# A hand-set order for TensorE in two attentions: what replacing a scheduler's order by set distances does to the time

## The chip, the cores and the metric

The kernel runs on one core of a Trainium2 chip. The metric is the device time of one execution in microseconds. Before the change it is 2630.18 us, the median of three runs (2629.49 to 2632.86). The profile shown below was taken of one further execution, which took 2629.03 us; the stretch from its first to its last instruction, the span, is 2627.2 us.

## The reference, cut to what matters

Two blocks of two layers each work on 512 latent tokens and 256 context tokens of width 1024. Only the first block's two attentions are touched by the change. In short form:

```python
# layer 0: neighborhood attention, 16 heads of 64
q, k = rms_norm(q, q_gain), rms_norm(k, k_gain)           # per head
s = concat(q @ k_window.T * dh**-0.5 + rpb_bias, q @ k_ctx.T * dh**-0.5)
y_lat = softmax(s) @ concat(v_window, v_ctx)              # 512 latent rows
y_ctx = softmax(q_ctx @ k_ctx.T * dh**-0.5) @ v_ctx       # 256 context rows

# layer 1: sliding window attention, 16 query heads on 4 key heads, with a sink
q, k = rope(rms_norm(q, g)), rope(rms_norm(k, g))
s = concat(where(|i - j| <= 128, q @ k.T, -1e30), q @ k_ctx.T, sink)
y_lat = softmax(s)[..., :-1] @ concat(v, v_ctx)
```

All of it is float32. Where a product needs more precision than one fast pass gives, a number is held as a high and a low part, and two or three fast products are summed.

## The kernel before, in words

Activations are kept with features on the partitions: `hl` (8 tiles of 128 features by 512 latent tokens) and `hc` (the same by 256 context tokens). After the norm their high and low parts are `uhl`, `ull`, `uhc`, `ulc`. A weight block arrives as `wraw` by DMA on SyncE's queue; `split` (L128, L129) makes `whi` on ScalarE and `wlo` on VectorE or, in the attentions, on GpSimd. A projection (`lin_steps`, L170; `tok_steps`, L180 for the values) is 24 products for a tile: high by high, high by low, and low by high. These are called dense products here, and their results are the tiles `mm`.

In the neighborhood attention the 16 heads are taken as 8 pairs (`hp`). `qk_proj` makes a pair's queries and keys in four tiles; `head_norm` squares a tile on ScalarE (L341), sums the squares with the matrix `blk` on TensorE into the tile `NS` (L344), takes logarithm, exponential and a square on ScalarE (L345, L346, L348), multiplies on GpSimd (L349) and corrects on VectorE (L350 to L352). There is one bank for `NS`, so the next `NS` product waits until L350 has read the last one. A pair has five blocks of 128 query rows (block 4 is the context), each for two heads; one such unit is `unit`: four score products into `S` (L391, L392), a softmax on VectorE and ScalarE (L358, L698 to L700), four transposes of the weights into `PT` (L704), and a copy into `pts` (L707 on ScalarE or L709 on VectorE). There is one `PT` bank. `attend` (L725) then makes the value products into `ST`, eight for a block.

In the sliding window attention `proj(t)` makes the queries of head pair `t`, `head_norm` follows, and `rope` turns them: a product with the matrix `rot` into the same `NS` bank (L820), which reads what L352 wrote. A unit here has scores against up to three blocks of keys (`SL`) and against the context (`SC`, one bank for both heads), a softmax (L358, L880 to L882), transposes into `PT` (L887), copies on ScalarE (L888), and value products (L904).

The order on every engine was set by the framework's scheduler. It takes instructions by priority, which is the order of the code, as soon as its own model of durations says that they are ready; the hardware then executes each engine's list strictly in that order. Only the `ada` bursts (products of the modulation weights, tile `AD`) were pinned behind a score product by hand.

Of the kernel before, what the change touches and what calls it, by code (L numbers as in the profile page):

```python
# [12 lines left out]
F32 = mybir.dt.float32  # L13
# [49 lines left out]
def kernel(ctx: ExitStack, tc: tile.TileContext, A, out, stop_after=None):  # L63
# [130 lines left out]

    def wide_w(w, c, s, **kw):

        return load_w([(0, 512, w[512 * s:512 * s + 512, c:c + 512])], 4, 512, **kw)
# [34 lines left out]
    def ada_burst(i, burst):  # L232

        for which, k, raw in burst:
# [4 lines left out]
            if k == KD - 1:  # L239
                ada_done(i, which, scr["adps"])  # L240

    def ada_done(i, which, ps, b=None):
# [4 lines left out]
        pt = bank(tag)  # L247
        n = 2 * nb
        for m in range(2):
            nc.tensor.matmul(out=pt[:, n * m:n * m + n], lhsT=rows[:, 128 * m:128 * m + 128], rhs=sel[:, n - 4:2 * n - 4])  # L250
# [7 lines left out]
        o = VOFF[f"ada_b{i}"][0]  # L258
        for v in range(2):
            nc.vector.tensor_tensor(  # L260
                out=view(mod[i][:, :, v]), in0=pt[:, 0:2 * n].rearrange("p (m j v) -> p m j v", v=2, j=nb)[:, :, :, v],
                in1=view(vecs[:, o:o + 48]), op=ALU.add)
# [74 lines left out]
    def head_norm(ps, n, gain):  # L337

        sq, r, q = tmp(n), tmp(n), tmp(n)
        ps = ps[:, :n]  # L340
        nc.scalar.activation(out=sq, in_=ps, func=AF.Square)  # L341
        nc.vector.tensor_scalar(out=q, in0=ps, scalar1=gain, scalar2=None, op0=ALU.mult)  # L342
        st = ns_tile()[:, :n]
# [84 lines left out]
    with tc.tile_pool(name="first", bufs=1) as fp, scratch("scr1", 6, 2):  # L428
# [154 lines left out]
        def neighborhood():  # L583
# [4 lines left out]
            with tc.tile_pool(name="na", bufs=1) as ap_:  # L588
# [26 lines left out]
                def qk_w(hp, lo_eng=None):  # L615
                    return load_w([(0, 128, wqkv[:, 128 * hp:128 * hp + 128]),
                                   (128, 128, wqkv[:, D + 128 * hp:D + 128 * hp + 128])], KD, 256, lo_eng)
# [47 lines left out]
                v_proj(0)  # L665

                def unit(hp, e, b):
# [18 lines left out]
                    else:  # L686
# [13 lines left out]
                        nc.vector.tensor_scalar(out=p, in0=p, scalar1=rl, scalar2=None, op0=ALU.mult)  # L700
                    pt = bank("PT")
# [3 lines left out]
                    pts = ap_.tile([128, 512], F32, name="pts", tag="pts", bufs=3)  # L705
# [4 lines left out]
                    return pts  # L710

# [31 lines left out]
                for hp in range(8):  # L743
                    pv = bank("ST")
                    if hp == 7:
                        scr["lo"] = nc.vector
                        oh = (u_lat(), u_ctx())
                    for b in range(5):
                        if b == 1 and hp < 7:
                            qk_proj(hp + 1, qk_w(hp + 1))  # L750
                        if b == 1 and hp < 6:
                            v_proj(hp // 2 + 1, range(3, 6) if hp % 2 else range(3))
                        pair = [unit(hp, e, b) for e in range(2)]
                        if bursts and bursts[0][0] == (hp, b):
                            bursts.pop(0)
                            with tc.high_priority(offset=1000), tc.issue_after(scr["score"].ins):
                                ada_burst(0, loaded)
                            if bursts:
                                loaded = ada_loads(0, todo, [home(x) for x in bursts[0][1]])
                        if b == 4:  # L760
                            pc = bank("ST")
                            attend(hp, b, pair, pc)
                            if hp == 7:
                                back(oh[1], 7, slice(0, NCTX), pc[:, 0:NCTX])
                            else:
                                nc.scalar.activation(out=hc[:, hp, :], in_=pc[:, 0:NCTX], func=AF.Copy)
                        else:
                            attend(hp, b, pair, pv)
# [825 lines left out]
```

## Time and profile before

| what | us |
|---|---|
| median of three runs | 2630.18 |
| the profiled execution | 2629.03 |
| its span | 2627.2 |
| neighborhood attention, first transpose to last copy | 84 to 448 |
| sliding window attention, projections of keys and values | 1076 to 1124 |
| sliding window attention, first scores to last value products | 1124 to 1297 |

TensorE is busy in 97% of the span, VectorE in 62%, ScalarE in 48%, GpSimd in 12%. A view by stretches gives, for each engine, the busy time in that stretch and in brackets the count of instructions; `PEclk` is the share of full clock that TensorE was granted. PEld is the weight load, which runs beside the products. In a timeline a row is an instruction (or several alike, x4), with its start, its duration, and in square brackets the idle time of its engine before it and what ended that. A product's duration includes its way through the array, so two products follow each other faster than one of them lasts. A float32 product that isn't in the fast format shows as two records, so eight value products show as x16.

### The profile page before, as it was taken

What the parts mean: (1) busy time and instruction counts of PE and PEld (TensorE: products, weight loads), DVE (VectorE), ACT (ScalarE), POOL (GpSimd) and SP (SyncE); (2) the same over time, 40 slices, a digit from 0 to 9 for tenths busy, and PEclk for the clock granted to TensorE, in tenths of its full rate; (3) what the DMA queues carried; (4) which work ended last, traced back from release to release, by engine and by line L of the source; (5) the groups of instructions that cost most, each with busy time, mean ns of one, the idle gap of its engine ahead of it and who ended that gap; (6) DMA issues with size and microseconds to landing.
All of it is one profiled execution on the core that took longest, in us unless ns stands there. A gap on an engine that the chain in (4) does not pass through costs nothing.

```text
span 2627.2 us, 39778 instructions
## 1 busy us (share of the span) xinstructions
PE 2551.8 (97%) x15300; PEld 2161.6 (82%) x15300; DVE 1634.0 (62%) x3496; ACT 1248.7 (48%) x2614; POOL 315.4 (12%) x344
## 2 busy tenths in 40 slices
PE   7999999999999999999999999999999999999998
PEld 4877787888888889877798888988878788888887
DVE  5666778686666577788664444767754646533245
ACT  5555666432222223678652323456654655544342
POOL 2322210100000000342010000111100212101011
PEclk9999999999999999999999999999999999999999
DMA  9232213143333342210133333332223222322331
GB/s 286 89 97 78 72 53 95 57 153 111 116 114 123 101 129 65 71 39 17 33 97 97 97 96 96 85 81 75 62 84 88 76 76 84 98 92 94 98 96 51
DMA packets 211485, 237.85 MB, mean 91 GB/s; under 512 B 9824, under 2 KB 167008, under 8 KB 211296
## 3 DMA queue, kind: packets, MB, share of 16 engines
q1 hardware_dynamic: 204320, 229.15, 28.3%
q10 hardware_dynamic: 6976, 6.17, 0.8%
q8 instruction: 120, 1.97, 0.3%
q14 instruction: 69, 0.57, 0.1%
HBM read 233.18 MB, written 2.10 MB: 90 GB/s over the span
## 4 chain that ended last, share of the span: by engine, by line
PE 82%; DVE 10%; ACT 5%; issue 2%; POOL 0%; DMA 0%; POOLq 0%; ACTq 0%; DVEq 0%
PE mm L170 60%; PE mm L180 7%; DVE t L325 2%; PE ST L725 2%; PE PT L704 2%; PE ST L904 1%; PE PT L887 1%; DVE acc L313 1%; DVE wlo L129 1%; PE S L391 1%; PE NS L344 1%; PE S L392 1%; DVE p L358 1%; PE PO L1146 1%; DVE t L972 1%
## 5 line engine op out<-in xcount | busy, mean ns | idle before, releaser
L129 DVE TENSOR_TENSOR wlo<-wraw,whi 128x512 fp32r<-128x512 f32 (+1 forms) x580 | 390.8, 712 | 307.0 <-ACT whi L128 210.7
L170 PE MATMUL mm<-uhl,whi 128*128 128x512 f32 (+1 forms) x1480 | 573.2, 391 | 3.3 <-DVE hc L463 2.1
L128 ACT ACTIVATE whi<-wraw 128x512 fp32r<-128x512 f32 (+1 forms) x632 | 354.8, 619 | 421.9 <-PE mm L170 233.6
L170 PE MATMUL mm<-ull,whi 128*128 128x512 f32 (+1 forms) x1480 | 552.0, 385 | 0.5 <-POOL ull L129 0.5
L170 PE MATMUL mm<-uhl,wlo 128*128 128x512 f32 (+1 forms) x1480 | 376.9, 383 | 1.8 <-DVE wlo L129 1.5
L170 PEld LDWEIGHTS mm<-uhl,whi 128*128 128x128 f32 x1480 | 278.9, 189 | 57.4 <-issue 3.5
L170 PEld LDWEIGHTS mm<-uhl,wlo 128*128 128x128 f32 x1480 | 273.5, 188 | 54.1 <-DVE wlo L129 2.8
L170 PEld LDWEIGHTS mm<-ull,whi 128*128 128x128 f32 x1480 | 273.4, 189 | 49.5 <-issue 3.0
L170 PE MATMUL mm<-h1l,whi 128*128 128x512 f32 (+1 forms) x576 | 208.0, 368 | 0.0
L170 PE MATMUL mm<-h1h,whi 128*128 128x512 f32 (+1 forms) x576 | 207.7, 368 | 0.0
L463 DVE SCALAR_TENSOR_TENSOR hl<-mm,mod,hl 128x512 f32<-128x512 f32 (+1 forms) x156 | 105.2, 679 | 160.4 <-PE mm L170 160.1
L129 POOL TENSOR_TENSOR ull<-t,uhl 128x256 fp32r<-128x256 f32 (+1 forms) x40 | 37.8, 949 | 1077.7 <-ACT uhl L128 988.3
L170 PE MATMUL mm<-h1h,wlo 128*128 128x512 f32 (+1 forms) x576 | 140.4, 366 | 0.0
L519 ACT ACTIVATE t<-mm 128x512 f32<-128x512 f32 (+1 forms) x100 | 50.5, 505 | 188.5 <-PE mm L170 188.5
L180 PE MATMUL mm<-whi,uhl 128*128 128x256 f32 (+1 forms) x448 | 137.8, 330 | 2.1 <-DVE t L342 1.5
L276 DVE SCALAR_TENSOR_TENSOR aacc<-araw,csil,aacc 128x512 f32<-128x512 f32 x196 | 136.2, 743 | 0.0
L180 PE MATMUL mm<-whi,ull 128*128 128x256 f32 (+1 forms) x448 | 135.3, 324 | 0.0
L170 PEld LDWEIGHTS mm<-h1h,whi 128*128 128x128 f32 x576 | 108.8, 189 | 16.9 <-ACT whi L128 0.6
L170 PEld LDWEIGHTS mm<-h1l,whi 128*128 128x128 f32 x576 | 108.9, 189 | 16.1
L170 PEld LDWEIGHTS mm<-h1h,wlo 128*128 128x128 f32 x576 | 101.7, 189 | 17.6
L170 PE MATMUL mm<-uhc,whi 128*128 128x256 f32 x448 | 111.5, 285 | 1.0 <-ACT uhc L128 0.8
L524 DVE TENSOR_TENSOR t<-mm,t 128x512 f32<-128x512 f32 (+1 forms) x96 | 55.2, 576 | 85.9 <-ACT t L519 85.3
(386 smaller groups left out, 5138.4 us busy)
## 6 DMA issues: line engine op xcount, KB each, us to landing
wraw<-mlp_w SPq DMA_DIRECT2D x128, 512.0 KB, 4.2
wraw<-l_w_in SPq DMA_DIRECT2D x88, 512.0 KB, 3.9
araw<-ada_w SPq DMA_DIRECT2D x112, 256.0 KB, 2.9
wraw<-l_w_out SPq DMA_DIRECT2D x32, 512.0 KB, 3.5
wraw<-l_w_in SPq DMA_DIRECT2D x48, 256.0 KB, 3.4
wraw<-na_wqkv SPq DMA_DIRECT2D x32, 256.0 KB, 3.4
hl<-ada_w SPq DMA_DIRECT2D x14, 512.0 KB, 5.0
wraw<-swa_wqkv SPq DMA_DIRECT2D x12, 512.0 KB, 4.0
```

The costliest lines, as they stand in the source:

```text
L128: nc.scalar.activation(out=hi, in_=src, func=AF.Copy)
L129: lo_eng.tensor_tensor(out=lo, in0=src, in1=hi.bitcast(F32), op=ALU.subtract)
L170: nc.tensor.matmul(out=o[0], lhsT=a[:, i, ms], rhs=o[j][:, i, :], start=(start and n_ == 0), stop=(stop and n_ == len(terms) - 1))
L180: nc.tensor.matmul(out=ps, lhsT=x[:, i, :], rhs=w[:, i - k0, :], start=(k0 == 0 and n_ == 0), stop=(k1 == KD and n_ == len(terms) - 1))
L276: nc.vector.scalar_tensor_tensor(out=acc[v], in0=raw, scalar=x, in1=acc[v], op0=ALU.mult, op1=ALU.add)
L313: nc.vector.tensor_tensor(out=acc, in0=acc, in1=sq, op=ALU.add)
L325: nc.vector.scalar_tensor_tensor(out=t, in0=h, scalar=gain, in1=r, op0=ALU.mult, op1=ALU.mult)
L463: nc.vector.scalar_tensor_tensor(out=o, in0=ps, scalar=mod[i][:, 8 * which + m, v:v + 1], in1=h, op0=ALU.mult, op1=ALU.add)
L519: nc.scalar.activation(out=a, in_=p, func=AF.Relu)
L524: nc.vector.tensor_tensor(out=q, in0=p, in1=a, op=ALU.mult)
L704: nc.tensor.transpose(pt[:, o:o + 128], p[:, 128 * c:128 * c + 128], ident)
L725: nc.tensor.matmul(out=o[64 * e:64 * e + 64], lhsT=vt[:, c, vo[e]:vo[e] + 64], rhs=pair[e][:, s], start=(j == 0), stop=(j == len(steps) - ...
```

## The change

Inside both attentions TensorE's order is now the order in which the code emits its instructions (`manual_schedule` for TensorE alone). The other engines are still ordered by the scheduler. A class `Weave` counts dense products in units of a 512-column product and runs steps when their position is reached. In the neighborhood attention a pair takes 111 units (73 in the last one that is woven, which has no value projection): the scores of block b stand at 22b and 22b+3, their transposes at 22b+19 and 22b+23, the value products of blocks 0 and 1 together at 62.9, of 2 and 3 at 106.9, and of block 4 at 128.9, in the next pair. A norm's `NS` product comes 8 units after its projection. The weights of the projection after next are loaded at 75, into the room of those just used. The last pair is still left to the scheduler. `pts` has four buffers in place of three.

In the sliding window attention a head pair takes 28 units: 24 of its projection, and 4 in which no dense product runs. A block takes 7; transposes follow 9.5 units behind their scores, value products of two blocks at 16.4. The `NS` product comes 3 units after the projection (in part in the 4 empty ones), and `rot` 8 units after that. The context's value projection is woven with the first projection of queries.

```diff
+    class Weave:
+        def __init__(self):
+            self.u, self.steps, self.n = 0.0, [], itertools.count()
+        def at(self, pos, f):
+            heapq.heappush(self.steps, (pos, next(self.n), f))
+        def later(self, d, f):
+            self.at(self.u + d, f)
+        def run(self, dense):
+            for n in dense:
+                self.u += (n + 32) / 544
+                self.emit(self.u)
+        def emit(self, u=math.inf):
+            while self.steps and self.steps[0][0] <= u:
+                heapq.heappop(self.steps)[2]()
...
+                            W.later(8, lambda j=j, v=v, t=t: norm(j, v, t))
...
+                    for b in range(5):
+                        for e in range(2):
+                            at(22 * b + 3 * e, S, b, e)
+                            at(22 * b + 19 + 4 * e, T, b, e)
+                        if (hp, b) in [x for x, _ in bursts]:
+                            at(22 * b + 8, burst)
+                    for bs, x in (((0, 1), 62.9), ((2, 3), 106.9), ((4,), 128.9)):
+                        at(x, PV, bs)
...
+                    if hp < 6:
+                        at(75, lambda: qkw.append(qk_w(hp + 2, room=qkw[0])))
+                    if hp < 6 and hp % 2 == 0:
+                        at(1, lambda: v_w(hp // 2 + 1))
...
+                with tc.manual_schedule(engines={mybir.EngineType.PE}):
+                    for hp in range(7):
+                        dense = [proj(hp + 1, qkw[-1])]
+                        pair_steps(hp, 1.0 if hp < 6 else 73 / 111)
+                        if hp < 6:
+                            dense.append(v_tiles(hp // 2 + 1, range(3, 6) if hp % 2 else range(3)))
+                        W.run(itertools.chain(*dense))
+                    W.emit()
...
+                def proj(t, d1=3, d2=8):
...
+                    def turn(q32):
+                        rope(q32, LAT)
+                        q_out(t, q32)
+                    def norm():
+                        q32 = head_norm_end(NLAT, *x)
+                        W.later(d2, lambda: turn(q32))
+                    W.later(d1, norm)
+                    if t:
+                        for _ in range(4):
+                            yield 512
...
+                with tc.manual_schedule(engines={mybir.EngineType.PE}):
+                    W.run(itertools.chain(proj(0, 5, 20), v_tiles(NLAT, NCTX, parts(uc, CTX))))
...
+                for t in range(8):
+                    for b in range(4):
+                        x = u0 + 16 + 28 * t + 7 * b
+                        for e in range(2):
+                            W.at(x + 3.5 * e, lambda t=t, b=b, e=e: S(t, b, e))
+                            W.at(x + 9.5 + 3.5 * e, lambda t=t, b=b, e=e: T(t, b, e))
+                        if b % 2:
+                            W.at(x + 16.4, lambda t=t, b=b: PV(t, (b - 1, b)))
+                with tc.manual_schedule(engines={mybir.EngineType.PE}):
+                    for t in range(1, 8):
+                        W.run(proj(t))
+                    W.emit()
```

How this moves instructions is shown at three places. The first is TensorE in the neighborhood attention, where a new pair begins. Before, the scheduler put the scores of a new pair one behind the other, with few dense products between them, and waited with them until that pair's norms were through:

```order
L391 MATMUL S<-ky,qx 128x256
L392 MATMUL S<-ky,ql_121 128x256
L170 MATMUL mm<-uhl,whi 128x512
L170 MATMUL mm<-ull,whi 128x512
L170 MATMUL mm<-uhl,whi 128x512
L170 MATMUL mm<-ull,whi 128x512
L170 MATMUL mm<-uhl,whi 128x512
L170 MATMUL mm<-ull,whi 128x512
L391 MATMUL S<-ky,qx 128x256
L392 MATMUL S<-ky,ql_121 128x256
L391 MATMUL S<-ky,qx 128x256
L392 MATMUL S<-ky,ql_121 128x256
```

Now, at the start of a pair, the value products of two blocks of the pair before (`ST`) and its last transposes (`PT`) come first, then the new scores, and behind them long runs of dense products:

```order
L765 MATMUL ST<-pts,vt 64x128 x16
L741 MATMUL PT<-ident,p 128x128 x4
L181 MATMUL mm<-wlo,uhc 128x256 x7
L741 MATMUL PT<-ident,p 128x128 x4
L181 MATMUL mm<-wlo,uhc 128x256
L171 MATMUL mm<-uhl,whi 128x512
L424 MATMUL S<-ky,qx 128x256
L425 MATMUL S<-ky,ql_120 128x256
L424 MATMUL S<-ky,qx 128x256
L425 MATMUL S<-ky,ql_120 128x256
L171 MATMUL mm<-ull,whi 128x512
L171 MATMUL mm<-uhl,whi 128x512
```

What moved: the attention of a pair, which stood in one cluster followed by a long dense stretch, is spread over the whole pair, and the norms of the next pair end long before its first scores.

The second place is TensorE in the sliding window attention, between the `NS` product of a norm (`blk`) and the turning product (`rot`) that reads the norm's result. Before, in the fifth head pair, six groups of scores and eight value products stand there, in part left out here:

```order
L344 MATMUL NS<-t_12280,blk 128x512
L887 MATMUL PT<-ident,p 128x128 x4
...
L904 MATMUL ST<-pts,vt 64x128 x8
L391 MATMUL SL<-ky_10751,qx 128x384
...
L170 MATMUL mm<-uhl,whi 128x512
L170 MATMUL mm<-ull,whi 128x512
L820 MATMUL NS<-t_12282,rot 128x512
```

Now, in the same way for each head pair from the second on, eight dense products, nine transposes and two groups of scores (four products each, of which the first is shown) stand between:

```order
L377 MATMUL NS<-t_11642,blk 128x512
L171 MATMUL mm<-uhl,whi 128x512
L1038 MATMUL PT<-ident,p 128x128 x4
L171 MATMUL mm<-ull,whi 128x512
L424 MATMUL SL<-ky_10738,qx 128x384
...
L171 MATMUL mm<-uhl,whi 128x512
L1038 MATMUL PT<-ident,p 128x128 x5
L171 MATMUL mm<-ull,whi 128x512
...
L171 MATMUL mm<-uhl,whi 128x512
L939 MATMUL NS<-t_11644,rot 128x512
```

The value products that stood there have moved in front of the `NS` product.

The third place is ScalarE between the same two products. Before, in the head pair shown, the norm's three steps had two copies among them and no softmax:

```order
L345 ACTIVATE t_12281<-NS,eps 128x512
L888 COPY pts<-PT 128x256 x2
L346 ACTIVATE t_12281<-t_12281 128x512
L348 ACTIVATE t_12280<-t_12281 128x512
L880 ACTIVATE p,rl<-p,nm 128x641 x2
```

Now a softmax exponential (`p,rl`) and a copy stand among them:

```order
L378 ACTIVATE t_11643<-NS,eps 128x512
L1028 ACTIVATE p,rl<-p,nm 128x641
L379 ACTIVATE t_11643<-t_11643 128x512
L1039 COPY pts<-PT 128x256
L381 ACTIVATE t_11642<-t_11643 128x512
L1039 COPY pts<-PT 128x256
```

The scheduler, which still orders this engine, put the exponential of a unit that is ready by then ahead of the norm's second step.

## Rows read from the trace of the kernel before

**Rows 1.** The page's head: busy time of the engines

```profile
PE 2551.8 (97%) x15300; PEld 2161.6 (82%) x15300; DVE 1634.0 (62%) x3496; ACT 1248.7 (48%) x2614; POOL 315.4 (12%) x344
```

**Rows 2.** By stretch: busy us (count) of each engine, granted clock, DMA

```profile
84.00:388.00 304.00, 288.55 (x2209) 239.51 (x2209) 209.01 (x540) 178.64 (x416) 69.81 (x58) 0.99 0.26 81
388.00:452.00 64.00, 60.39 (x454) 49.18 (x451) 55.71 (x163) 44.46 (x110) 4.59 (x4) 0.97 0.26 81
...
1150.00:1276.00 126.00, 122.89 (x969) 95.23 (x969) 109.68 (x344) 103.06 (x250) 31.82 (x61) 1.00 0.09 26
```

**Rows 3.** TensorE's waits, 84 to 388: in total, times, longest

```profile
PE S L391 <- DVE nm L358: 7.2, 6, 2.6
```

**Rows 4.** Timeline of TensorE at the start of a pair

```profile
169.47 0.39 PE L391 MATMUL S<-ky,qx 128*128 128x256 f32 x1 [2.63 <-DVE nm L358]
...
169.81 0.28 PE L391 MATMUL S<-ky,qx 128*128 128x256 f32 x1
...
170.95 0.41 PE L391 MATMUL S<-ky,qx 128*128 128x256 f32 x1
```

**Rows 5.** Timelines of VectorE and GpSimd just before

```profile
164.68 2.58 POOL L129 TENSOR_TENSOR wlo<-wraw,whi 128x512 fp32r<-128x512 f32 x2 [2.03 <-ACT whi L128]
...
164.72 1.41 DVE L351 TENSOR_SCALAR t<-t 128x256 f32<-128x256 f32 x1
...
167.47 0.41 DVE L358 CUSTOM_DVE_ANT_0 p<-S,bias 128x256 f32<-128x256 f32 x1
```

**Rows 6.** Timeline, a norm and its turning with nothing beside them

```profile
1114.24 1.12 PE L344 MATMUL NS<-t,blk 128*128 128x512 f32 x2 [0.69 <-ACT t L341]
...
1115.03 0.57 PE L170 MATMUL mm<-uhl,whi 128*128 128x512 f32 x1
...
1115.43 0.39 PE L170 MATMUL mm<-ull,whi 128*128 128x512 f32 x1
...
1115.66 0.40 PE L170 MATMUL mm<-uhl,whi 128*128 128x512 f32 x1
...
1117.45 0.69 DVE L350 SCALAR_TENSOR_TENSOR t<-NS,t 128x512 f32<-128x512 f32 x1 [2.48 <-ACT t L348]
...
1118.25 0.43 DVE L351 TENSOR_SCALAR t<-t 128x512 f32<-128x512 f32 x1
...
1119.45 1.13 PE L820 MATMUL NS<-t,rot 128*128 128x512 f32 x2
```

**Rows 7.** Timeline, the same among attention, fifth head pair

```profile
1191.60 1.02 PE L344 MATMUL NS<-t,blk 128*128 128x512 f32 x2
...
1192.46 0.60 PE L887 MATMUL PT<-ident,p 128*128 128x128 f32 x4
...
1192.82 0.42 PE L391 MATMUL SL<-ky,qx 128*128 128x384 f32 x1
...
1193.25 0.64 ACT L888 COPY pts<-PT 128x256 f32<-128x256 f32 x2
...
1193.56 0.62 DVE L358 CUSTOM_DVE_ANT_0 p<-SL,wmask,sink 128x384 f32<-128x384 f32 x1 [0.78 <-PE SL L392]
...
1194.69 0.44 PE L391 MATMUL SL<-ky,qx 128*128 128x384 f32 x1
...
1194.99 0.82 ACT L880 ACTIVATE p<-p,nm 128x641 f32<-128x641 f32 x1
...
1195.37 0.34 PE L391 MATMUL SL<-ky,qx 128*128 128x384 f32 x1
...
1195.71 0.18 ACT L880 ACTIVATION_READ_ACCUMULATOR p<-p,nm 128x1 f32 x1
...
1196.60 0.16 DVE L881 RECIPROCAL rl<-rl 128x1 f32<-128x1 f32 x1
...
1198.17 1.02 PE L820 MATMUL NS<-t,rot 128*128 128x512 f32 x2
```

**Rows 8.** Copies of transposed weights, 84 to 452: ns shortest/median/longest

```profile
L709 DVE COPY pts<-PT x48: 678/690/693, 85.2 to 448.0; 128x512 f32<-128x512 f32 x48
```

More of the change, by code (lines that the diff above doesn't have):

```diff
@@ L1 @@
+import heapq
 import itertools
@@ L239, in ada_burst, with ada_done @@
             if k == KD - 1:
-                ada_done(i, which, scr["adps"])
-    def ada_done(i, which, ps, b=None):
+                later(10, ada_done(i, which, scr["adps"], now=False))
+    def ada_done(i, which, ps, b=None, now=True):
         nb = 4 if b is None else 2
@@ L256, in view, with rest @@
             return t[:, 8 * which:8 * which + 16].rearrange("p (j m) -> p m j", m=8)[:, 2 * b:2 * b + 2, :]
[L258 to L262, printed above, removed]
+        def rest():
+            pt = bank(tag)
+            for m in range(2):
+                nc.tensor.matmul(out=pt[:, n * m:n * m + n], lhsT=rows[:, 128 * m:128 * m + 128], rhs=sel[:, n - 4:2 * n - 4])
+            o = VOFF[f"ada_b{i}"][0]
+            for v in range(2):
+                nc.vector.tensor_tensor(
+                    out=view(mod[i][:, :, v]), in0=pt[:, 0:2 * n].rearrange("p (m j v) -> p m j v", v=2, j=nb)[:, :, :, v],
+                    in1=view(vecs[:, o:o + 48]), op=ALU.add)
+        if not now:
+            return rest
+        rest()
     def ada_vector(i, which, half, pool):
@@ L665, in neighborhood, with scores @@
                 v_proj(0)
-                def unit(hp, e, b):
+                wq1 = qk_w(1, nc.gpsimd)
+                def scores(hp, e, b):
                     q, k = qks[hp]
@@ L710, in unit @@
                     return pts
+                def unit(hp, e, b):
+                    return transposed(b, scores(hp, e, b))
                 def back(o, k, c, x):
@@ L742, in neighborhood @@
                 loaded = ada_loads(0, todo, [home(x) for x in bursts[0][1]])
[L743 to L747, printed above, removed]
-                    for b in range(5):
[L749 to L768, printed above, removed]
-                        if b == 3:
-                            for c, x in ((slice(64, NLAT), pv[:, 0:NLAT - 64]), (slice(0, 64), pv[:, NLAT - 64:NLAT])):
-                                if hp == 7:
-                                    back(oh[0], 7, c, x)
-                                else:
-                                    nc.scalar.activation(out=hl[:, hp, c], in_=x, func=AF.Copy)
-                    for h in range(2 * hp + 3, min(2 * hp + 3 + 2, 16)):
-                        load_bias(h)
-                    if hp == 7:
-                        ws = [load_w([(0, 256, A["na_wo"][:, 256 * x:256 * x + 256])], KD, 256) for x in range(1)]
@@ new lines, in neighborhood @@
+                scr["lo"] = nc.vector
+                oh = (u_lat(), u_ctx())
+                pv = bank("ST")
+                for b in range(5):
+                    pair = [unit(7, e, b) for e in range(2)]
+                    if b == 4:
+                        pc = bank("ST")
+                        attend(7, b, pair, pc)
+                        back(oh[1], 7, slice(0, NCTX), pc[:, 0:NCTX])
+                    else:
+                        attend(7, b, pair, pv)
+                    if b == 3:
+                        heads_out(7, pv)
@@ L779, in neighborhood @@
+                ws = [load_w([(0, 256, A["na_wo"][:, 256 * x:256 * x + 256])], KD, 256) for x in range(1)]
                 for k in range(7):
```

157 lines of the change are left out of this document (120 added, 37 removed).

## The prediction

> **What bounds the kernel now.** I read the page's head first, then the busy time by stretch, then TensorE's waits and their places in the timeline. TensorE is busy for 2551.8 us, 97% of the span [rows 1], so a new order can give back only idle time, time at the lower clock, and what it costs to change between the fast format and plain float32. By stretch [rows 2], the neighborhood attention has 304.0 - 288.55 = 15.45 us idle up to 388 and 64.0 - 60.39 = 3.61 in its last two pairs. The granted clock is 0.99 and 0.97 there: at half speed in part of the stretch, which costs 0.01 x 304 + 0.03 x 64, about 5 us. So about 24 us could be had in the first attention. In the steady part of the sliding window attention it is 126.0 - 122.89 = 3.1 us. There VectorE is busy for 109.68 of 126 us, 87%, and ScalarE for 103.06, 82%: that attention is close to three bounds at once.
>
> The largest single wait in the first attention is for VectorE's L358, 7.2 us in 6 waits [rows 3]. The longest of them lasts 2.63 us [rows 4]. VectorE worked there on the norm of the very pair whose scores had just begun: L351 at 164.72, and L358, which frees the score bank, only at 167.47 [rows 5]. The scores at 170.95 then last 0.41 us, the same product at 169.81 only 0.28: the lower of the two clocks, after that idle time.
>
> **The change part by part.** Counts of work stay: the same products, transposes and softmaxes. Runs of plain float32 work between runs in the fast format, counted in the two orders, go from 118 to 122 in the first attention and from 81 to 80 in the second. The value products of two blocks in a row thus save nothing: before, most of them already stood next to transposes. I take 0; at some 0.2 us for a change there and back it is at most 1 us either way.
>
> *First attention, what goes.* The scores of a pair now come about 30 units of 0.23 us after the last norm product of that pair, with attention work between, so the handover wait and its half-clock stretch go. Of the 24 us all but what is newly late goes.
>
> *First attention, what is late next.* Two things in each of the six full pairs. One is the single `NS` bank: the second norm of a tile pair stands 4.4 to 4.9 us after the first, by the work that the new order puts between. Alone, the chain from the `NS` product to the end of L350 takes 1118.14 - 1114.24 = 3.9 us [rows 6]. With one exponential (0.82 us [rows 7], a little wider than here) among the ScalarE steps it is 4.7, and with VectorE's scaling of that unit in front of L350, some 5.2. So TensorE waits 0 to 0.8 us, twice a pair. The other is the single `PT` bank: the second transposes of a block stand 1.5 to 2.3 us after the start of the first, and between lie about 0.7 us until these are through and a copy of 0.69 [rows 8]. That fits if the copy starts at once; behind one or two other VectorE or ScalarE steps it is 0.5 late, in perhaps two of five blocks. Together 1.8 us in a pair, 11 us for six. The compressed pair and the unwoven last one keep the 5.5 us that they lose now (3.61 idle, 1.9 of clock), and I add 1.5 because the compressed pair asks VectorE for the same work in less time: 7. So 18 of 24 us stay lost: **-6 us**. Bounds: -18 if the late copies and norms hide, +2 if both are late everywhere.
>
> The row for this shows one more thing: L351 took 1.41 us at 164.72 on half of the columns, against 0.43 for all of them at 1118.25 [rows 5, 6], while GpSimd made `wlo` at 164.68. [...]
>
> *Weights and queues.* The loads move with their DMAs on SyncE's queue: the projection after next at position 75, into the room of the one just used. From there to the next pair lie 36 units of dense work and the attention between, some 16 us; GpSimd's four splits take 2 x 2.58 = 5.2 [rows 5], where two take 2.58. That covers it; if it failed it would cost what is over 16 us, which I take as 0. The bursts' data were fetched three blocks earlier before and still are.
>
> *Second attention, the rotation.* `rot` reads what L352 wrote. TensorE's work from the start of the `NS` product to `rot` is now: `NS` 0.79 (1114.24 to 1115.03 [rows 6]), eight dense products at 0.23, 1.84 (1115.43 to 1115.66), two groups of scores at 0.68 less their change of format, 1.2 (1194.69 to 1195.37 [rows 7]), nine transposes at 0.09 (four in 0.36, 1192.46 to 1192.82), 0.8, and some 0.5 for five changes of format: 5.1 us. The chain that `rot` waits for takes 1119.45 - 1114.24 = 5.2 us with nothing beside it [rows 6], and 1198.17 - 1191.60 = 6.6 us among attention [rows 7], where ScalarE had only copies between the norm's steps. The new order has an exponential there in five of the seven head pairs (0.82, 0.90 with the readout that ends at 1195.89) and one or two copies of 0.4, and on VectorE a group of scores (0.62) and a reciprocal (0.16) ahead of L352: 5.2 + 0.9 + 0.4 + 0.8 = 7.3 us. TensorE, which must keep the order, waits 7.3 - 5.1 = 2.2 us in each of 7 head pairs: +15.5. The bounds are 6.6 - 5.1 = 1.5, thus +10.5, and 3 each, +21, if VectorE at 87% has a queue in front of it. Nothing else uses the wait on TensorE: the transposes and scores queued behind `rot` are ready and cannot pass it.
>
> *Second attention, what is saved.* VectorE catches up during these waits, so the 3.1 us of steady idle go. Two waits of 0.69 us for a norm's first square (one at 1114.24 [rows 6]) go, since that norm is now woven: 1.4. The beginning has 3.0 us between the first scores and their transposes, where softmax needs about as much, and the tail runs without dense work in both orders: I take 0 and 1 us. Sum: 15.5 - 3.1 - 1.4 + 1 = **+12 us**, from +4 to +19.
>
> **Sum.** -6 + 12 = +6 us against the profiled execution of 2629.03: 2635. That execution lay 1.15 us below the median of the runs, so the median should be 2636.
>
> **The rivals.**
> *Faster: the spread order hides what I call late.* If the copies and second norms come in time, the first attention gains 18; if the exponential on ScalarE slips behind the norm, the wait at `rot` is 1.5 us, 10.5 - 3.1 - 1.4 = +6 and, with the tail's waits gone, +4. Then 2629 - 18 + 4 + 1 = 2616. For it speaks that the first attention's losses stand at handovers which the new order removes outright; against it that the chain of 5.2 us has no slack even alone. It wins once a pair of the first attention loses less than 0.5 us.
> *No change.* Each term halfway: -10 and +9, 2630 for the median. Nothing but the sizes decides between this and the forecast.
> *Much slower: the lower clock.* After the wait of 2.63 us the clock was low [rows 4]. If half of the seven waits at `rot` are followed by such a stretch, at 1.7 us each (the 5 us above are three of them), that is 6 more: 2642. [...]
>
> **How the numbers follow.** Forecast (slower, 2636) 0.32; much slower 0.15; no change 0.28; faster 0.25. About 0.2%, 5 us, is what a measurement of this kernel can tell from no change. The forecast's own range is 2631 to 2641, of which a part lies inside 0.2%: I count 0.04 of it there and as much of the middle case beyond it. So slower 0.47, the same 0.28, faster 0.25. The range from 2617 to 2648 leaves out the best part of the faster case and waits of more than 3 us at `rot`.
>
> **What would show it.** In the changed profile, waits of TensorE before `rot` for L352's counterpart, seven of about 2 us, and VectorE's share below 87% in the steady part: right. Waits there under 0.7 us: the second attention's term is wrong. In the first attention, TensorE's wait for scores at handovers must be gone; idle time there by stretch of about 13 us and more confirms my 18 with the clock, 6 or less makes the faster rival right.

## The result, and the profile after the change

The changed kernel takes 2652.58 us, the median of five runs (2650.57 to 2654.73), against 2630.18 before: a ratio of 1.0084, 95% interval 1.007 to 1.0098. It is slower by 22.4 us; the forecast was 2636, its range ended at 2648.

The two traces can be laid side by side at places with the same dense work. The first product of the MLP behind the first attention starts at 577.54 us before and at 586.07 after: **the first attention costs 8.5 us more**. From there to the first such product behind the second attention it is 805.07 us before and 817.43 after: **the second costs 12.4 us more**. The rest differs by 1.4.

By stretch (stretch, length; busy us and count of PE, PEld, DVE, ACT, POOL; granted clock, DMA share, GB/s), what answers to [rows 2]:

```profile
84.00:388.00 304.00, 278.02 (x2156) 240.71 (x2155) 202.06 (x528) 175.49 (x410) 68.07 (x58) 0.96 0.25 77
388.00:452.00 64.00, 59.55 (x437) 48.67 (x435) 56.66 (x164) 43.98 (x106) 4.57 (x4) 1.00 0.25 81
...
1150.00:1276.00 126.00, 113.94 (x893) 90.23 (x888) 99.98 (x310) 95.25 (x231) 27.38 (x58) 0.99 0.06 18
```

Up to 388 TensorE is idle for 26.0 us, not 15.45, and its clock is 0.96, not 0.99. The waits of TensorE from 84 to 460 (us in total, times, longest), where [rows 3] had the score bank first:

```profile
PE PT L741 <- ACT pts L744: 20.7, 6, 4.5
PE NS L377 <- DVE t L383: 4.0, 4, 1.3
PE PT L741 <- DVE pts L746: 2.6, 6, 0.8
```

The wait for scores at the handover is gone, and in its place stands one wait in each of the six full pairs, for a copy by ScalarE. One of them, followed back through the timelines of the engines (start, duration, idle time before and its releaser):

```profile
213.59 4.13 POOL L130 TENSOR_TENSOR wlo<-wraw,whi 128x512 fp32r<-128x512 f32 x3 [6.29 <-PE mm L171]
217.69 1.28 POOL L382 TENSOR_TENSOR t<-t,t 128x512 f32<-128x512 f32 x1
218.93 1.29 POOL L130 TENSOR_TENSOR wlo<-wraw,whi 128x512 fp32r<-128x512 f32 x1
...
219.00 1.50 DVE L384 TENSOR_SCALAR t<-t 128x512 f32<-128x512 f32 x1 [1.41 <-POOL t L382]
220.53 1.09 DVE L385 TENSOR_TENSOR t<-t,t 128x512 f32<-128x512 f32 x1
...
221.66 1.28 ACT L418 ACTIVATE ky<-t 64x512 fp32r<-64x512 f32 x2 [2.23 <-DVE t L385]
222.96 0.58 ACT L744 COPY pts<-PT 128x512 f32<-128x512 f32 x1
...
219.71 0.28 PE L424 MATMUL S<-ky,qx 128*128 128x256 f32 x1
...
223.60 1.12 PE L741 MATMUL PT<-ident,p 128*128 128x128 f32 x4 [3.01 <-ACT pts L744]
...
225.37 0.42 PE L424 MATMUL S<-ky,qx 128*128 128x256 f32 x1
```

Read it from the bottom. TensorE waits 3.01 us for the one PT bank, which the copy L744 empties. The copy is ready long before, but on ScalarE it stands behind L418, which waits for the keys' norm (L385 on VectorE). That waits for the norm's product L382 on GpSimd, and on GpSimd three weight splits stand ahead of it, 4.13 us. Of the 3.0 us, about half is the queue (VectorE is idle for 1.41 us until L382 is through), and half is VectorE itself, beside GpSimd's work: L384 takes 1.50 us and L385 1.09, where they take 0.43 and 0.69 alone (at 94.79 and 95.25). After the wait the score product lasts 0.42 us, not 0.28: TensorE is at a lower clock for a while (granted clock 0.50 from 223.5 to 226).

The waits from 1076 to 1310, in the second attention, the longest of the kernel before and then those of the changed one:

```profile
PE PT L887 <- DVE p L882: 2.0, 4, 0.7
PE NS L344 <- ACT t L341: 1.4, 2, 0.7
PE NS L820 <- DVE t L352: 0.9, 3, 0.3
```

```profile
PE NS L939 <- DVE t L385: 10.5, 10, 2.5
PE PT L1038 <- ACT pts L1039: 4.8, 10, 1.4
PE SC L424 <- DVE nm L391: 2.5, 7, 1.0
PE SL L424 <- ACT qx L410: 2.4, 1, 2.4
```

L939 is `rot`, L820 before. The seven waits before it in the woven pairs are 0.94, 1.49, 2.50, 1.49, 0.85, 1.47 and 0.89 us, 9.6 together.

### The profile page after: what moved, and what is told of

Its sections match the earlier page's. It is cut to its first block, busy times and chain, and to the rows that moved or that the text cites. A ratio compares the mean times of both kernels' runs of the same rounds, so it can differ in the third digit from the quotient of the medians.

```text
span 2649.5 us, 39766 instructions
## 1 busy us (share of the span) xinstructions
PE 2546.7 (96%) x15300; PEld 2172.8 (82%) x15300; DVE 1637.2 (62%) x3496; ACT 1249.1 (47%) x2614; POOL 312.5 (12%) x344
## 4 chain that ended last, share of the span: by engine, by line
PE 81%; DVE 10%; ACT 5%; issue 2%; POOL 1%; DMA 1%; SPq 0%; POOLq 0%; DVEq 0%; ACTq 0%
PE mm L171 60%; PE mm L181 8%; PE PT L741 1%; DVE t L352 1%; PE PT L1038 1%; PE ST L1063 1%; DVE wlo L130 1%; DVE p L391 1%; PE ST L765 1%; DVE acc L340 1%; PE S L425 1%; PE NS L377 1%; PE S L424 1%; PE AD L231 1%; PE PO L1321 1%
## 5 line engine op out<-in xcount | busy, mean ns | idle before, releaser
L130 DVE TENSOR_TENSOR wlo<-wraw,whi 128x512 fp32r<-128x512 f32 x576 | 388.4, 713 | 306.4 <-ACT whi L129 210.4
L171 PE MATMUL mm<-uhl,whi 128*128 128x512 f32 (+1 forms) x1464 | 567.0, 391 | 4.1 <-DVE hc L496 2.1
L129 ACT ACTIVATE whi<-wraw 128x512 fp32r<-128x512 f32 x628 | 353.1, 619 | 426.1 <-PE mm L171 234.5
L171 PE MATMUL mm<-ull,whi 128*128 128x512 f32 (+1 forms) x1464 | 550.1, 388 | 0.5 <-POOL ull L130 0.5
L171 PE MATMUL mm<-uhl,wlo 128*128 128x512 f32 (+1 forms) x1464 | 375.8, 384 | 1.8 <-DVE wlo L130 1.5
L171 PEld LDWEIGHTS mm<-uhl,whi 128*128 128x128 f32 x1464 | 275.5, 189 | 57.7 <-ACT whi L129 4.0
L171 PEld LDWEIGHTS mm<-uhl,wlo 128*128 128x128 f32 x1464 | 270.9, 188 | 54.0 <-DVE wlo L130 2.8
L171 PEld LDWEIGHTS mm<-ull,whi 128*128 128x128 f32 x1464 | 270.3, 189 | 49.2 <-issue 3.5
L171 PE MATMUL mm<-h1l,whi 128*128 128x512 f32 (+1 forms) x576 | 208.3, 369 | 0.0
L171 PE MATMUL mm<-h1h,whi 128*128 128x512 f32 (+1 forms) x576 | 207.9, 368 | 0.0
L171 PE MATMUL mm<-h1h,wlo 128*128 128x512 f32 (+1 forms) x576 | 140.4, 366 | 0.0
L171 PEld LDWEIGHTS mm<-h1h,whi 128*128 128x128 f32 x576 | 108.9, 189 | 16.8 <-ACT whi L129 0.8
L171 PEld LDWEIGHTS mm<-h1l,whi 128*128 128x128 f32 x576 | 109.0, 189 | 16.0
L171 PEld LDWEIGHTS mm<-h1h,wlo 128*128 128x128 f32 x576 | 101.8, 189 | 17.5
L171 PE MATMUL mm<-uhc,whi 128*128 128x256 f32 x448 | 112.2, 285 | 1.0 <-ACT p L715 0.7
L171 PE MATMUL mm<-ulc,whi 128*128 128x256 f32 x448 | 109.2, 286 | 0.3 <-DVE ulc L130 0.3
```

The source lines that it names most:

```text
L129: nc.scalar.activation(out=hi, in_=src, func=AF.Copy)
L130: lo_eng.tensor_tensor(out=lo, in0=src, in1=hi.bitcast(F32), op=ALU.subtract)
L171: nc.tensor.matmul(out=o[0], lhsT=a[:, i, ms], rhs=o[j][:, i, :], start=(start and n_ == 0), stop=(stop and n_ == len(terms) - 1))
```

## The experiments

Every run's ratio is to the kernel before on the same chip, with its 95% interval. Where a run is taken apart by attention, the places are those used above, in its one profiled execution.

**One part alone.** The first attention as before, the second as after.

> The neighborhood attention is ordered as before the change, the sliding window attention as after it. Theory A (the two parts are independent, and the losses stand where the two traces part: 8.5 us in the first attention, 12.4 in the second): 2630.2 + 12.4 = 2643, within 2 us. Rival (the second attention is slow because of what the first leaves behind, or the rest is in places outside both): under 2638 or over 2647.

2642.91 us, 1.0050 (1.0037 to 1.0063), +12.8. That is near the 12.4 that the traces give to the second attention, so the parts add up and each can be studied by itself.

**Splits on VectorE.**

```diff
-at(75, lambda: qkw.append(qk_w(hp + 2, room=qkw[0])))
+at(75, lambda: qkw.append(qk_w(hp + 2, nc.vector, room=qkw[0])))
```

> As after the change, but in the neighborhood attention the low parts of the query and key weights are made on VectorE, not on GpSimd; nothing else changes, and TensorE's order is the same. Theory Q (GpSimd's queue: the norm's product L382 of the keys stands behind up to three splits there, VectorE's L384 and L385 wait for it, ScalarE's L418 waits for these, and the copy L744 stands behind L418, so TensorE waits for it with 20.7 us in six waits and a lower clock behind each): those waits fall under 6 us, the granted clock of 84 to 388 goes from 0.96 to 0.98 or more, time 2626 to 2636. Rival S (ScalarE's order alone makes the copy late, whoever makes the splits): 2648 to 2656. Rival V (VectorE becomes the bound with the added 2.8 us a pair): waits for L746 and for L391 grow, 2640 or more.

2618.24 us, 0.9955 (0.9942 to 0.9969): 34 us less than the changed kernel by one argument, more than I expected. Stretch and waits:

```profile
84.00:388.00 304.00, 299.12 (x2385) 257.39 (x2385) 230.34 (x630) 195.76 (x465) 43.58 (x36) 1.00 0.27 83
```

```profile
PE PT L741 <- DVE pts L746: 2.6, 6, 0.8
PE NS L377 <- DVE t L383: 2.3, 4, 0.8
```

The waits for L744 are not merely shorter, they are gone; idle time falls from 26.0 to 4.9 us, the clock is 1.00, and VectorE, with more to do, holds TensorE up no more than it did. Theories S and V fall.

**The norm's product on VectorE, splits on GpSimd as after the change.**

```diff
-nc.gpsimd.tensor_tensor(out=q, in0=q, in1=r, op=ALU.mult)      # L382
+scr.get("nm", nc.gpsimd).tensor_tensor(out=q, in0=q, in1=r, op=ALU.mult)
...
+scr["nm"] = nc.vector
```

> As after the change, but the norm's product L382 of the woven neighborhood attention is made on VectorE, while the splits stay on GpSimd. Theory Q: L382 no longer waits behind splits, so the six waits for L744 fall from 20.7 to under 8 us; VectorE's L384 beside GpSimd's splits may still take 1.5 us in place of 0.43, so a part of the delay stays: 2630 to 2640. Rival S: 2648 to 2656. Rival P (the slow VectorE steps beside GpSimd's splits are the cause, not the queue): waits for L744 stay over 14 us, 2645 to 2655.

2637.61 us, 1.0024 (1.0015 to 1.0034). It takes 15 of the 34 us, and the time is where theory Q had it. What is left:

```profile
PE PT L741 <- ACT pts L744: 9.0, 7, 2.2
PE NS L377 <- DVE t L383: 6.5, 5, 1.5
PE PT L741 <- DVE p L734: 3.1, 3, 2.1
```

So the queue is one cause and not the only one: VectorE's steps are still slow while GpSimd splits beside them (L385 on 512 columns takes up to 1.78 us, against 0.69 alone).

**The same load, asked for later** (position 92 for 75).

> As after the change, splits on GpSimd as there, but the query and key weights of the projection after next are asked for at position 92 of a pair and not at 75, so that the splits come after the norms of the keys. Theory Q+P (the loss is that splits and the keys' norm meet in time, on GpSimd's queue and beside VectorE): the six waits for L744 fall under 6 us and the time comes near that with the splits on VectorE, 2617 to 2628. Rival D (then the weights themselves are late for the next pair's first products): a wait of mm for wlo of 1 us or more in each pair, 2630 or more. Rival S (ScalarE's order): 2648 to 2656.

2653.97 us, 1.0090 (1.0076 to 1.0103): nothing. The run tests nothing either: the scheduler put every split and every DMA where it had stood, so that all engines' lists were the same in both attentions. A split moves up to where its room becomes free, behind the last product that reads the old weights ("<-PE mm L171" at 213.59 above), whatever position asks for it.

**The splits held behind the last norm of the pair on GpSimd.**

```diff
+def next_w():
+    with tc.issue_after(scr["nm"].ins):       # the last L382
+        qkw.append(qk_w(hp + 2, room=qkw[0]))
-at(75, lambda: qkw.append(...))
+at(92, next_w)
```

> As after the change, splits on GpSimd, but in GpSimd's list the four splits of the next query and key weights stand behind the product L382 of the last norm of the pair (in the run with the later position the scheduler had left every engine's list as it was, so that run did not test this). Theory Q (the queue is the loss): the waits for L744 fall from 20.7 to under 4 us, 2617 to 2624. Theory Q+P (queue and slow VectorE steps beside the splits share the loss): the splits now run beside other VectorE work, waits for L746 and L734 grow to 4 us or more, 2624 to 2632. Rival D (the weights come late): waits of mm for wlo in each pair, 2632 or more.

2626.66 us, 0.9993 (0.9984 to 1.0002), 26 of the 34 us. The time is in the range of theory Q+P (queue and slow steps share the loss); the waits for L744 fall as theory Q said, and those for L746 grow less than Q+P did. Waits:

```profile
PE PT L741 <- DVE pts L746: 3.4, 9, 0.8
PE PT L741 <- ACT pts L744: 3.1, 5, 0.7
PE NS L377 <- DVE t L383: 2.5, 3, 1.3
```

No weights are late. With the queue in order the same splits on the same engine cost some 8 us, not 34 (10 by the ratios): they must be made somewhere, and beside them VectorE is slower (L385 on 256 columns 1.40 us, against 0.43 at 223.83 in the changed kernel).

**All copies of transposed weights on VectorE**, so that none stands behind L418.

```diff
-if b % 2:
+if b % 2 and not dve:
     nc.scalar.copy(out=pts, in_=pt)
```

> As after the change, splits on GpSimd, but all copies of transposed weights in the woven neighborhood attention are made on VectorE, so none stands behind L418 on ScalarE. Theory Q with its chain (L382 late, then L385, then L418, then the copy): the copy is now behind L385 or beside it on VectorE itself, which waits for the same L382; some of the loss stays, 2632 to 2645. Rival S (ScalarE's order alone): the 20.7 us and the lower clock go, 2618 to 2626.

2639.31 us, 1.0043 (1.0030 to 1.0055), 13 of the 34 us. The wait changes its name: L746 holds TensorE for 15.3 us in 11 waits. ScalarE's order is one link of the chain, not its beginning.

**The kernel before, with its splits on VectorE.**

```diff
-qk_proj(hp + 1, qk_w(hp + 1))
+qk_proj(hp + 1, qk_w(hp + 1, nc.vector))
```

> The kernel before the change, but with the low parts of the query and key weights of the neighborhood attention made on VectorE. Theory H (before, the first attention lost its time at the handover of pairs, where a norm's VectorE steps were slow beside the splits, but the single scores wait stays when the order stays): a part goes, 2620 to 2628. Rival O (the engine of the splits is all, and the hand-set order gives nothing): as low as with the hand-set order in the first attention alone, 2604 to 2612. Rival N (VectorE is fuller at the handovers): 2630 to 2636.

2622.48 us, 0.9974 (0.9964 to 0.9984), as theory H said, some 7 less than before. The wait for scores at the handover is shorter but stays (84 to 460, the kernel before and this run):

```profile
PE S L391 <- DVE nm L358: 8.7, 7, 2.6
PE S L391 <- DVE nm L358: 5.1, 5, 1.6
```

**The first attention alone, with splits on VectorE**; the second ordered as before.

> The neighborhood attention ordered by hand with the weight splits on VectorE (as in the run with the splits on VectorE, 2618.2), the sliding window attention ordered as before the change. Theory A (the parts are independent; the second attention's new order costs 12.4 to 12.8 us): 2618.2 - 12.6 = 2605.6, within 2.5 us. Rival: the first attention's gain comes back later: over 2610.

2606.96 us, 0.9913 (0.9900 to 0.9927). Against the run above this is what the change does to the first attention when neither kernel splits these weights on GpSimd: 2622.5 - 2607.0 = 15.5 us gained. With splits on GpSimd the same change loses 8.5. The earlier load and the fourth `pts` buffer are in both figures; no run separates them from the order.

**Single value products**, in both attentions, on top of the splits on VectorE.

```diff
-for bs, x in (((0, 1), 62.9), ((2, 3), 106.9), ((4,), 128.9)):
+for bs, x in (((b,), 22 * b + 40.9) for b in range(5)):
...
-if b % 2:
-    W.at(x + 16.4, lambda t=t, b=b: PV(t, (b - 1, b)))
+W.at(x + 16.4, lambda t=t, b=b: PV(t, (b,)))
```

> As the run with the splits on VectorE (2618.2), but each block's value products stand by themselves in both attentions (at 22b + 40.9 in the first, at 16.4 behind the scores in the second), not two blocks in a row. Theory Z (as predicted: two blocks in a row save nothing to speak of): 2618 within 3 us. Rival G (each change between the fast format and plain float32 costs some 0.2 us and about 35 more of them are made): 2622 to 2628.

2619.91 us, 0.9964 (0.9951 to 0.9976), 1.7 above the run with two in a row and inside its uncertainty. But that is the sum of two differences. The first attention ends 5.2 us later than there (the first product of the MLP at 558.86, against 553.67; 553.3 to 556.0 in the ten runs with the rows of two and the splits on VectorE). The second is 3.1 us shorter (813.92 against 816.99; 817.0 to 820.4 in the seven runs with the change's own order there): TensorE is idle in it for 21.0 us, not 26.1. So the rows of two are worth about 5 us in the first attention, and in the second they cost more in waits than they save.

**Second attention: `rot` later** (as after the change otherwise).

```diff
-def proj(t, d1=3, d2=8):
+def proj(t, d1=3, d2=12):
-x = u0 + 16 + 28 * t + 7 * b
+x = u0 + 20 + 28 * t + 7 * b
```

> As after the change, but in the sliding window attention the turning product (rot) comes 12 units after the norm's product, not 8, and the scores, transposes and value products of all pairs come 4 units later. Theory R (rot stands too near behind the norm: 9.6 us in seven waits): these fall under 2 us, the first wait for scores (2.4 us) goes, the tail is longer by 1 to 2: 2641 to 2646. Rival B (VectorE at 79% and ScalarE at 76% set the pace of this stretch, and the wait only moves): waits for transposes, score banks or stacked queries take its place, 2650 to 2656.

2652.23 us, 1.0081 (1.0068 to 1.0093): theory R falls. The waits at `rot` are gone, as it said, and the time of the whole is the same (in the profiled execution the second attention's part is 1.7 us shorter, about as much as such parts differ between runs of the same order). What stands first now:

```profile
PE SC L424 <- DVE nm L391: 8.3, 15, 1.4
PE PT L1038 <- ACT pts L1039: 7.1, 14, 2.4
```

**More room**: four buffers of softmax rows in place of three, transposes at 13 (9.5) and value products at 19.9 (16.4), on top of the splits on VectorE.

> As the run with the splits on VectorE (2618.2), but in the sliding window attention the softmax rows have four buffers, not three, transposes stand 13 units behind their scores, not 9.5, and value products 19.9, not 16.4. Theory L (the fixed order gives softmax too little time, so that each late step on VectorE or ScalarE holds TensorE): waits for transposes and for rot shrink, 2608 to 2614. Rival K (the single banks SC and NS and the norm's chain hold it whatever the distance of the transposes): 2616 to 2622.

2620.74 us, 0.9968 (0.9957 to 0.9980): no gain over 2618.24; SC alone holds TensorE for 14.0 us in 18 waits.

**SC's halves in turn**: one tile for the whole attention, not one for each block (`if t == b == e == 0:` for `if e == 0:`), with `rot` at 12.

> As the run with the splits on VectorE (2618.2), with rot at 12 units and the attention 4 units later (which alone changed nothing), and the two halves of the context scores' bank SC are used in turn, each free as soon as its own head's L391 has read it, not both together. Theory C (SC's release is the limit next behind rot): waits for SC fall from 8.3 us to under 2, 2607 to 2612. Rival B (VectorE and ScalarE set the pace): the wait moves to transposes or scores again, 2615 to 2620.

2615.67 us, 0.9951 (0.9939 to 0.9964), and with more room as well:

> As the run before, and also four buffers of softmax rows, transposes 13 units behind their scores, value products 19.9. Theory C with latency: all waits of this stretch under 5 us together, 2604 to 2610. Rival B: 2615 to 2620.

2616.73 us, 0.9954 (0.9941 to 0.9968). Neither tests SC's release, since the halves aren't released separately. In the first of the two:

```profile
1131.46 0.34 PE L424 MATMUL SL<-ky,qx 128*128 128x384 f32 x1
...
1132.26 0.48 DVE L391 CUSTOM_DVE_ANT_0 p<-SC,zero,nm 128x256 f32<-128x256 f32 x1
...
1132.81 0.38 PE L424 MATMUL SC<-ky,qx 128*128 128x256 f32 x1 [0.84 <-DVE nm L391]
...
1133.44 0.48 DVE L391 CUSTOM_DVE_ANT_0 p<-SC,zero,nm 128x256 f32<-128x256 f32 x1
```

The product at 1132.81 writes the half that is read at 1133.44, and yet it waits, 0.84 us, for the read of the other half, which ends at about 1132.7. Whether the bank or the one tile of both halves is the reason, no run separates.

**A bank of its own for each head's context scores**, taken from SL (`SL="1", SC="23"`), with `rot` at 12.

> As the run with the splits on VectorE (2618.2), with rot at 12 units and the attention 4 units later, each head's context scores in a bank of their own by turns (two banks) and the scores of the window in one bank in place of two. Theory C (the release of SC sets the pace): waits for SC under 2 us, 2607 to 2612. Rival B (VectorE comes late to whichever bank is read): the waits stand at SL with the same sum of 7 us or more, 2614 to 2622.

2615.27 us, 0.9949 (0.9935 to 0.9962). The time is in rival B's range and the wait moves again, more of it to the transposes than to SL, where rival B had it:

```profile
PE PT L1038 <- ACT pts L1039: 8.7, 15, 2.1
PE SL L424 <- DVE nm L391: 4.5, 6, 1.8
```

**A step of VectorE left out**: the line of L1030 removed, so that the softmax rows are not divided by their sums.

> As the run with the splits on VectorE (2618.2), with the softmax rows of the sliding window attention left undivided by their sums (this part of the computation is left out; about 4.4 us of VectorE's work in each head pair of some 23 us). Theory B (VectorE's work and its place in the chain set the pace): TensorE's waits in this stretch fall by half or more, 2604 to 2611. Rival C or the distances alone: 2614 to 2619.

2611.77 us, 0.9931 (0.9919 to 0.9944), 6.5 less than with it, between the two expectations. VectorE's busy time from 1114 to 1240 falls from 100.6 to 83.2 us, SC's waits vanish, and `rot` still has

```profile
PE NS L939 <- DVE t L385: 8.6, 7, 1.7
```

So VectorE's work is not the pace by itself: in that stretch alone it has 17 us less to do, and the whole gains 6.5.

**The scheduler free in the second attention** from the second pair on, code and so priorities in the new order (`if True:` for `with tc.manual_schedule(...)`), on top of the splits on VectorE.

> As the run with the splits on VectorE (2618.2), but in the sliding window attention from the second head pair on the scheduler is again free to order TensorE; the code emits its instructions in the new order. Theory F (it is the fixed list that costs, since the scheduler's list lets TensorE go on with what is ready): most of the 12.4 us come back, 2606 to 2612. Rival E (the order in which the code emits, thus the distances, costs whatever the scheduler does with it): 2616 to 2624.

2610.76 us, 0.9929 (0.9917 to 0.9942): 7.5 us back, as theory F said. In this run, from 1040 to 1290,

```profile
PE SL L424 <- ACT qx L410: 3.5, 4, 2.4
PE PT L1038 <- ACT pts L1039: 2.6, 4, 0.7
...
PE NS L939 <- DVE t L385: 0.9, 3, 0.3
```

no wait of note is left but the one for the first scores, 2.4 us.

**The best of both, tried.** The run above with SC's halves in turn and the first turning product 6 units earlier:

> As the run in which the scheduler orders TensorE in the second attention (2610.8), with SC's halves in turn and the first turning product 6 units earlier. The wait of 2.4 us for the first scores goes, and SC has only 1.2 us of waits there: 2607 to 2609. Rival (the first scores wait for something else in line): 2610 to 2613.

2608.43 us, 0.9922 (0.9910 to 0.9935). And the first attention alone with splits on VectorE, with SC's halves in turn:

> As the run with the hand-set order in the first attention alone and the splits on VectorE (2607.0), with SC's halves in turn in the second attention, whose order is the scheduler's. SC's waits there were 0.7 us: 2605 to 2608. Rival B': with SC free earlier the scheduler packs the attention closer and VectorE, at 87%, decides: 2608 to 2612.

2606.62 us, 0.9917 (0.9903 to 0.9930). The fastest versions, this one and 2606.96, cannot be told apart: about 0.9% under the kernel before. Both have the new order in the first attention and the scheduler's in the second.

## Why the prediction was right in direction and wrong in size

**The first attention: forecast -6, measured +8.5.** This is nearly the whole error, 14.5 of 16.4 us. The step that failed is the one on weights and queues: "That covers it; if it failed it would cost what is over 16 us, which I take as 0." It asked whether the splits end in time for the next pair, and they do. It did not ask what stands behind them on GpSimd. With the load one pair ahead and into the room of the weights just used, the splits become possible just when the last key product is done, which is when the keys' norms need GpSimd for L382 and VectorE for L384 and L385. The copy, which I had 0.5 us late in two of five blocks, is 3.0 to 4.5 us late once a pair: 20.7 us. Moving only the splits removes it all (34 us with the lower clock that follows), ordering GpSimd's list removes 26 of them, moving L382 removes 15.

What I had seen of GpSimd, L351 at 1.41 us beside a split [rows 5], I left out of the sum. L384 takes 1.50 us beside a split above and at most 0.43 with the splits on VectorE.

**The lower clock.** I had it as a rival, at `rot`. It came in the first attention: from 80 us to the first product of the MLP the clock cost 5.1 us before and 11.9 after (half of the 10.2 and 23.9 us in which the granted clock is 0.50), behind each of the six long waits. Of the seven waits at `rot` one was followed by it.

**The handover wait** went as forecast. The waits for the single `NS` bank, forecast at 0 to 0.8 us twice a pair, are 4.0 us in 4. Idle time and clock from 80 us to the MLP account for 11.2 + 6.8 = 18.0 us of loss where 8.5 are measured. So about 9 us were gained in TensorE's busy time, which I had at 0.

**Two in a row saves nothing**: wrong in the first attention, where it is worth about 5 us, 3 to 4 of them in TensorE's busy time. My count took transposes and value products as one format, and so it stays near 120 in both orders. But runs of value products alone go from 40 to 26, and a transpose behind one does not spare the change: in the kernel before, from the last record of a run of eight value products to the next instruction it is 0.20 us whether a transpose or a dense product follows, and 0.10 from one value product to the next inside a run. On the way in, from a dense product of 512 columns, it is 0.32 to 0.33, and 0.23 from one such product to the next; so there and back costs some 0.2 us, as I had it. Where the other 5 to 6 us of busy time were gained stays open.

**The second attention: forecast +12, measured +12.4, and 12.8 by itself.** Waits at `rot` were forecast at seven of 2.2 us, 15.5 together, and are seven of 1.4 us, 9.6: just under the lower bound of 10.5. What came on top I had not: 4.8 us at transposes, 2.4 at the first scores. And the 1.4 us that I saw saved at two first squares are still lost (1.2 us at L377). Between the two places of comparison TensorE is idle for 26.4 us, not 11.3, and loses 1.7 to the clock: 16.8 us, of which its shorter busy time gives 4.4 back. So that 12 came out as 12.4 is luck in part: a term at `rot` that was too large, waits that I had not, and a gain in busy time that I had not either. The bounds were not what the terms give: 10.5 and 21 at `rot`, with the other terms as they stand, make +7 and +17.5, not +4 and +19. The reading behind the term was wrong in one point, too. The sum treats the wait as a matter of the distance between `NS` and `rot`; with `rot` 4 units later most of it stands at SC and at the transposes. Where TensorE may take other ready work, 7.5 of the 12 us come back. So that much is the price of the fixed list. My reading of it, which no run isolates, is that in each pair ScalarE and VectorE run late somewhere, and the list has nothing else to offer TensorE there. Which of their chains is late first is not settled: another bank, later transposes and more buffers each gave under 3 us, less work for VectorE 6.5. The other 4 to 5 us (2610.8 against 2607.0 with the scheduler's own order) are in part the start, where 2.4 us wait for the first queries.

**The sum.** Slower, but by 22.4 us where 6 were forecast, outside the range. That the direction came out is the second attention's doing; the first was forecast faster and came out slower. The faster rival had -18 for the first attention, for a pair that loses under 0.5 us. With the splits off GpSimd the first attention gains more, 577.54 - 553.67 = 23.87 us, of which the kernel before gains 577.54 - 569.70 = 7.84 by the same move; and yet TensorE is still idle for 4.9 us in some six pairs, 0.8 each, so it does not win by its own condition. The sign for the forecast, idle time of 13 us and more, came with 26.0 + 4.5 us and would have confirmed a term whose mechanism was another: it had no upper end.

## What to carry to other kernels

When a step is moved, write down for each engine it uses what will stand behind it in that engine's list, not only whether it ends in time: a cheap split ahead of a norm's product held four engines in a row. A hand-set order for one engine is worth what the others' lists allow; set the lists of those that feed it too, or move their bulk work off the chain, and compare at that point. In the second attention, where VectorE and ScalarE have little room, the fixed list cost time, and a wait that was removed at one place turned up at the next. And look at each part of the kernel before calling a change worth nothing: single value products lost 5 us in one attention and gained 3 in the other.

## What the runs showed of the hardware

L384 and L734, steps of VectorE that read and write SBUF, didn't lose a share of their speed beside GpSimd but ended just behind GpSimd's instruction: L384 takes 1.50 us from 219.00, and the split beside it ends at 220.22, 0.28 us before the step does. In the changed kernel from 80 to 460 us, 18 steps of L384 and L734 on 512 columns began while GpSimd was at a split or at L382. All end 0.28 or 0.29 us behind that instruction, whether they take 0.70 or 1.51 us (alone 0.41 to 0.49). The four that began before GpSimd's instruction took no longer than alone. L383, which reads PSUM, takes 0.68 us at 216.51 beside a split, as without one.

The length of a wait did not by itself say whether a lower clock followed. At `rot` (first two rows the one, the last two the other wait):

```profile
1168.66 2.08 PE L939 MATMUL NS<-t,rot 128*128 128x512 f32 x2 [1.49 <-DVE t L385]
1169.75 1.42 PE L171 MATMUL mm<-ull,whi 128*128 128x512 f32 x1
...
1194.29 1.13 PE L939 MATMUL NS<-t,rot 128*128 128x512 f32 x2 [2.50 <-DVE t L385]
1194.85 0.80 PE L171 MATMUL mm<-ull,whi 128*128 128x512 f32 x1
```

The wait of 1.49 us is followed by products at the lower clock (granted 0.52 from 1168.5 to 1172; the dense product takes 1.42 us), the longer one of 2.50 us is not (1.00 from 1175 to 1200; 0.80 us). Nor is a wait of the same 1.49 us at 1217.57 (1.00 from 1200 to 1225), after which that product takes 0.80 us as well.
